# Two blocks of mixed rows turned into row tiles before the input projection ends, and the output projection and second norm in another order of blocks

## The chip, the core and the metric

The kernel runs on one NeuronCore of one Trainium2 chip. The metric is device time in microseconds: the median of repeated executions (three are shown). A separate execution was recorded by the hardware profiler; it shows when each instruction ran on each engine: TensorE (PE, matmuls; its weight loads are shown apart as PEld), VectorE (DVE), ScalarE (ACT), GpSimd (POOL), and SyncE (SP), whose queue starts the DMAs.

## What is computed

One decoder layer on 1024 tokens of width 1024. Cut to its steps:

```python
h = rms_norm(x, norm1_w)
da_q, da_k, da_v, dn_qkv, dn_z, dn_a, dn_b = split(h @ w_in)
# group A: differential attention, 4 heads, causal, two 64-wide softmax maps per head
p = softmax(scale * rms_norm(da_q) @ rms_norm(da_k).T + causal)        # for each of two maps
da_o = rms_norm((p[0] - lam * p[1]) @ da_v, da_out_norm_w) * (1 - lam_init)
# group B: gated DeltaNet, 4 heads: conv + SiLU, decay, chunked delta rule (a scan over the tokens)
dn_o = rms_norm(gated_delta_rule(...), dn_out_norm_w) * silu(dn_z)
mix = concat([da_o, dn_o], axis=-1)                                    # 512 + 512 columns
x = x + mix @ w_out
h = rms_norm(x, norm2_w)
x = x + square(relu(h @ w_up)) @ w_down
```

## The kernel before

Tokens are cut into eight blocks of 128 (`NT`), columns into eight of 128 (`KB`). Float32 products are made of three faster ones: each operand is split into a rounded high half and a low half that holds the rest, and each product runs as high x high, high x low, low x high. That is why three matmul lines always stand together: L994 to L996 in the input projection of attention (`da_units`), L1273 to L1275 in the output projection (`half`), L1434 to L1436 in the MLP's up products.

The left operand is held transposed in two large tiles, `hH` and `hL` (high and low halves, all eight column blocks by all tokens). During the input projection they hold the normed input; afterwards the mixed rows (`mix`, turned) take their place, and after the output projection the rows normed for the MLP. So a column block of `hH` can be overwritten only once the input projection has read it for the last time.

From about 220 us to 620 us of the span, the scan, the attention projection, attention, the output projection and the second norm run interleaved. The order of PE's instructions is written out by a planner (`Interleave`, L40 to L117): each piece of work is a Python generator, a "stream" with a priority; the planner keeps a clock of its own, adds estimated durations, and at each step takes the first stream, in order of priority, whose next step is due. Smaller numbers go first: scan 0, output of the scan 1, loads of mixed rows 1.4, turning of mixed rows 1.5, turning of q and k pieces 1.6, attention values 2, scores 3, input projection 4, turning of normed rows (`backs`) 4.5, output projection 5, first up products 6. PE's order is fixed by this; the framework's scheduler orders the other engines and SP's queue.

The streams that matter here:

- **`da_units`** (input projection for attention, three passes over eight blocks). At the end of the last pass it loads the first quarter of w_out (rows 512 to 1023, columns 0 to 511), `pre`, then sets `state["proj"]`. `da_turns` turns the q and k pieces, 32 in all, counted in `state["turned"]`.
- **`scores`** and **`values`** (attention, in units of one head and one block). `scores` makes both maps' scores in PSUM, takes the maximum (DVE, L1135), the exponential (ACT, L1139) into a tile `pexp` of the pool `ae` (four buffers) or, every third, of `be`, and combines the maps (DVE, L1149). At most three scored units wait in `ready`. `values` transposes the result (L1171), multiplies it with v (L1183), norms it and stores it to `mixa_d`. Head 1 is scored up to block 3 until the projection is done (L1102). The order of units is head 0, head 1 by rising blocks, then heads 2 and 3 together by falling blocks. `state["scored"]` and `state["attn"]` mark the ends of the two streams.
- **`mix_loads`** and **`mixed`**: the scan's rows (`mixn_d`, columns 512 to 1023 of the mix) are loaded block by block into `mt` (two buffers), from block 7 down (`tiles`), transposed on PE (L252), rounded by ACT into `hH` (L261) and split by DVE into `hL` (L262). Then attention's rows (`mixa_d`, columns 0 to 511) likewise, each block when its four heads are stored. After the sixteenth turn, and when attention is done, buffers are given back and `state["free"]` is set.
- **`outproj`** starts when `state["proj"]` and `state["scan"]` are set. `half(kh, w, n, tb)` is twelve matmuls of 512 columns: block `tb`, input half `kh`, output half `n`, accumulated in one of two PSUM banks and added by DVE to the residual row `accs[tb]` (L1280), which was loaded from x. First pass: `kh` = 1 (scan's rows), n = 0 for all eight blocks, then n = 1. Second pass: `kh` = 0 (attention's rows); of the list `todo` the first entry whose rows have been turned is taken. Quarters of w_out are loaded by `load_unit` into two alternating sets of weight tiles; ACT rounds them and POOL splits them (L213, L214).
- **`norm2`** runs behind a block's second n half: it stores the row to `acc_d`, squares it on ACT (L1292), and scales it by DVE into a `pexp` buffer of `ae` (L1298). Before `free` only the first four entries of `tiles` may do so, and only once all is scored.
- **`backs`** turns normed rows once `free` is set (L252 with `hn` for the first four blocks, with a copy into a `kept` tile on ACT, L256, and a split on DVE, L259; `turn_b`, L1366, for the last four). `up_first` makes the first products of the MLP from the first four blocks. Its weights are loaded when the last n = 0 half of the second pass is done.

The residual rows, the kept rows and the first raw up weights share the eight buffers of one tag, "row" (`row_tile`), so each new one waits for the release of the one eight allocations before.

Of the kernel before, what the change touches and what calls it, by code (L numbers as in the profile page):

```python
# [9 lines left out]
F32 = mybir.dt.float32  # L10
# [8 lines left out]
P = 128  # L19
# [113 lines left out]
def tile_hymba_layer(  # L133
# [113 lines left out]
    def to_hT(src, tb, psp, tag, k0=0, nk=KB, keep=None, col=None):  # L247
        sl = slice(tb * P, (tb + 1) * P)
        for g in range(0, nk, 4):
# [4 lines left out]
            ks = slice(k0 + g, k0 + g + 4)  # L254
            if keep is not None:
                S.copy(keep, psv)  # L256
            if col is None:
                S.copy(hH[:, ks, sl], psv)
                V.tensor_tensor(hL[:, ks, sl], psv, hH[:, ks, sl].bitcast(F32), ALU.subtract)  # L259
            else:  # L260
                S.activation(hH[:, ks, sl], psv, AF.Copy, scale=col)  # L261
                V.scalar_tensor_tensor(hL[:, ks, sl], psv, col, hH[:, ks, sl].bitcast(F32), ALU.mult, ALU.subtract)  # L262
# [609 lines left out]
    def scan_out(c, Sold, yy):  # L872
# [40 lines left out]
        if c == NT - 1:  # L913
# [6 lines left out]
            for tb in tiles:  # L920
                accs[tb] = row_tile("acc")
# [8 lines left out]
    def prefetch_x(after):  # L930
        if state["scan"] and state["xs"] < NT:
            tb = state["xs"]
# [3 lines left out]

    late, accs, vts, v_at, qa_free = [], {}, {}, {}, [0.0] * 3
# [136 lines left out]
    ready = []  # L1074

    def scores():
# [6 lines left out]
        for u, (h, tb) in enumerate(order):  # L1083
# [18 lines left out]
            while h == 1 and tb >= 4 and not state["proj"]:  # L1102
                yield flow.now + 100, None
# [11 lines left out]
            pl = n // npc  # L1115
            pe, ssum = [], ap.tile([P, 2], F32, tag="ssum", name="ssum", bufs=4)
            mx = ap.tile([P, 2], F32, tag="mx", name="mx", bufs=4)
            for m in range(2):
# [18 lines left out]
                ep = pools["be"] if state["scan"] and npe % 3 == 0 else ae  # L1137
                e = ep.tile([P, SEQ], F32, tag="pexp", name="pexp")
# [13 lines left out]
            ready.append((h, tb, pe[0], ri, vt, t))  # L1152
# [4 lines left out]
    def values():  # L1157
        for _ in order:
            while not ready or ready[0][5] > flow.now:
                yield (flow.now + 100 if not ready else ready[0][5]), None  # L1160
            h, tb, pe, ri, vt, _t = ready[0]
# [47 lines left out]
    def turn(src, t, tb, k0, keep=None, col=None):  # L1209
        r = yield from flow.bank("px", at=t)  # L1210
        to_hT(src, tb, px, "px", k0, 4, keep, col)
# [12 lines left out]
    def mix_loads():  # L1224
        while not (pre and state["scan"]):
# [9 lines left out]
    def mixed():  # L1235
        while not state["proj"]:
            yield flow.now + 200, None
        for i in range(2 * NT):
            while not loads:
                yield flow.now + 50, None  # L1240
            mt, t, tb, k0 = loads.pop(0)
            yield from turn(mt, t, tb, k0, col=mw[:, 1:2] if k0 else mw[:, 0:1])
# [18 lines left out]
    def outproj():  # L1261
# [4 lines left out]
        def half(kh, w, n, tb):  # L1266
# [3 lines left out]
            ps = pf.tile([P, 512], F32, tag="pf", name="ps_op")  # L1270
            for k in range(4):
                kk = 4 * kh + k
                T.matmul(ps, hH[:, kk, sl], wh[:, k, :], start=(k == 0), stop=False)  # L1273
# [563 lines left out]
```

## Time and profile before

| | us |
|---|---|
| median of the three runs | 1226.28 |
| lowest, highest | 1226.03, 1226.78 |
| profiled execution, whole | 1228.35 |
| its span, first to last instruction | 1226.6 |
| busy in the span: PE, DVE, ACT, POOL | 1212.7, 849.7, 605.4, 120.7 |
| input projection's last matmul (L996) starts | 444.08 |
| first output-projection matmul (L1273) | 450.20 |
| first and last transposition of mixed rows (L252 from mt) | 445.65, 589.93 |
| last attention value matmuls (L1183) | 580.66 |
| last output-projection matmul (L1275) | 607.94 |

The profile was taken on one execution of its own, so times inside it are read against 1226.6 and differences are carried over to the median. Matmuls are pipelined: one is shown from its start to its modelled end, so neighbours overlap. A row of the timeline reads: start, duration, engine, line of the kernel, operation, what it writes from what it reads, shape, count, and in brackets the idle time of the engine just before, with what ended it. In the waits view a row is: who waited, for whom, total, times, longest.

### The profile page before, as it was taken

Reading aid. Unit: us, or ns where it says so; the run is one execution under the profiler, and the core shown is the slowest. Engines: PE = TensorE matmul, PEld = TensorE weight load, DVE = VectorE, ACT = ScalarE, POOL = GpSimd, SP = SyncE. Lnnn points to the kernel's source line nnn. Section 1 sums busy time; section 2 is a strip of 40 time slices with the busy share of each in tenths; the row PEclk is TensorE's granted clock in tenths of the full one; section 3 lists DMA queues with packets and bytes.
Section 4 is the critical chain, followed back from the end, with each engine's and each line's share of the span. In section 5 each row is a group of like instructions: output and inputs, shape, how many; then the busy total and the mean of one; then the engine's idle time right before and its main releaser. Section 6 shows DMA issues by size and latency. Waiting matters only on the chain.

```text
span 1226.6 us, 17630 instructions
## 1 busy us (share of the span) xinstructions
PE 1212.7 (99%) x6331; PEld 1028.6 (84%) x6331; DVE 849.7 (69%) x1445; ACT 605.4 (49%) x1173; POOL 120.7 (10%) x162
## 2 busy tenths in 40 slices
PE   9999999999999999999999999999999999999998
PEld 9988888898788888888788888888888888888887
DVE  7687788478868577766798554565577955786553
ACT  7565544234456555656566444454563333333331
POOL 0011110223332231212100000000000000000000
PEclk9999999999999999999999999999999999999999
DMA  6564442457755674334528433443279855433401
GB/s 229 163 187 129 115 128 83 123 157 242 231 164 176 183 243 137 109 84 144 183 86 282 163 123 137 172 172 137 103 250 345 330 187 184 162 103 103 137 35 69
DMA packets 160783, 199.04 MB, mean 162 GB/s; under 512 B 20960, under 2 KB 120632, under 8 KB 160696
## 3 DMA queue, kind: packets, MB, share of 16 engines
q1 hardware_dynamic: 160696, 197.92, 49.2%
q8 instruction: 50, 0.82, 0.3%
q14 instruction: 37, 0.30, 0.1%
HBM read 132.32 MB, written 65.56 MB: 161 GB/s over the span
## 4 chain that ended last, share of the span: by engine, by line
PE 91%; DVE 3%; DMA 2%; ACT 2%; issue 1%; POOL 0%; SPq 0%; ACTq 0%; POOLq 0%; DVEq 0%
PE X L1436 5%; PE X L1435 5%; PE X L1434 5%; PE X L1750 4%; PE X L1751 4%; PE X L1752 4%; PE ps_dn L221 4%; PE ps_dn L220 4%; PE ps_dn L219 4%; PE ps_qk L994 3%; PE ps_qk L996 3%; PE ps_qk L995 3%; PE Y L1436 3%; PE Y L1435 3%; PE Y L1434 3%; PE ps_o L1183 2%
## 5 line engine op out<-in xcount | busy, mean ns | idle before, releaser
L1353 ACT CAST hH<-ur 128x1024 fp32r<-128x1024 f32 x56 | 58.7, 1050 | 166.0 <-PE X L1751 79.1
L1354 DVE TENSOR_TENSOR hL<-ur,hH 128x1024 fp32r<-128x1024 f32 x56 | 68.3, 1223 | 78.6 <-ACT hH L1353 78.6
L1354 DVE TENSOR_TENSOR op<-raw,op 128x1024 fp32r<-128x1024 f32 x48 | 58.7, 1223 | 75.1 <-PE X L1435 42.1
L1750 PE MATMUL X<-hH 128*128 128x512 f32 x224 | 87.1, 389 | 0.0
L1751 PE MATMUL X<-hL,hH 128*128 128x512 f32 x224 | 87.1, 389 | 0.0
L1752 PE MATMUL X<-hH,hL 128*128 128x512 f32 x224 | 87.1, 389 | 0.0
L994 PE MATMUL ps_qk<-wH,hH 128*128 128x512 f32 x192 | 81.9, 427 | 0.7 <-ACT qn L1022 0.7
L995 PE MATMUL ps_qk<-wL,hH 128*128 128x512 f32 x192 | 75.3, 392 | 1.2 <-DVE wL L214 1.2
L219 PE MATMUL ps_dn<-hH,wH 128*128 128x512 f32 x192 | 75.9, 395 | 0.0
L220 PE MATMUL ps_dn<-hL,wH 128*128 128x512 f32 x192 | 75.6, 394 | 0.0
L996 PE MATMUL ps_qk<-wH,hL 128*128 128x512 f32 x192 | 75.5, 393 | 0.0
L221 PE MATMUL ps_dn<-hH,wL 128*128 128x512 f32 x192 | 75.4, 393 | 0.0
L1354 DVE TENSOR_TENSOR hL<-dw,hH 128x1024 fp32r<-128x1024 f32 x56 | 68.2, 1219 | 2.8 <-ACT hH L1353 2.7
L1353 ACT CAST op<-raw 128x1024 fp32r<-128x1024 f32 x48 | 50.5, 1052 | 34.7 <-PE Y L1436 19.9
L1353 ACT CAST hH<-dw 128x1024 fp32r<-128x1024 f32 x56 | 58.6, 1047 | 16.7 <-PE X L1752 5.2
L1139 ACT ACTIVATE pexp<-ps_sc,mx 128x128 f32<-128x128 f32 (+7 forms) x64 | 47.3, 741 | 26.3 <-DVE mx L1135 26.2
L577 DVE SCALAR_TENSOR_TENSOR cy<-cp,pv,cy 128x512 f32<-128x512 f32 x72 | 53.9, 748 | 8.4 <-ACT cy L575 7.5
L1135 DVE TENSOR_REDUCE mx<-ps_sc 128x1 f32<-128x128 f32 (+7 forms) x64 | 47.5, 754 | 14.2 <-PE ps_sc L1133 13.7
L1273 PE MATMUL ps_op<-wH,hH 128*128 128x512 f32 x128 | 53.6, 419 | 0.0
L1275 PE MATMUL ps_op<-wH,hL 128*128 128x512 f32 x128 | 50.3, 393 | 0.0
L1274 PE MATMUL ps_op<-wL,hH 128*128 128x512 f32 x128 | 50.0, 391 | 0.0
L1434 PE MATMUL Y<-hH,op 128*128 128x512 f32 x128 | 49.8, 389 | 0.0
(355 smaller groups left out, 3382.3 us busy)
## 6 DMA issues: line engine op xcount, KB each, us to landing
ur<-ud SPq DMA_DIRECT2D x28, 1024.0 KB, 5.0
raw<-in_w_up_dram SPq DMA_DIRECT2D x32, 512.0 KB, 3.8
dw<-in_w_down_dram SPq DMA_DIRECT2D x32, 512.0 KB, 7.2
qk_d<-qa SPq DMA_DIRECT2D x32, 256.0 KB, 2.7
ud<-ua SPq DMA_DIRECT2D x16, 512.0 KB, 4.0
ud<-s SPq DMA_DIRECT2D x16, 512.0 KB, 2.6
wraw<-in_w_in_dram SPq DMA_DIRECT2D x24, 256.0 KB, 3.3
wraw<-in_w_in_dram SPq DMA_DIRECT2D x48, 128.0 KB, 2.6
```

The source lines that it names most:

```text
L219: T.matmul(ps, lh(k), rh(k), start=(k == 0), stop=False)
L220: T.matmul(ps, lh(k), rl(k), start=False, stop=False)
L221: T.matmul(ps, ll(k), rh(k), start=False, stop=(k == n - 1))
L994: T.matmul(ps, hH[:, 4 * kh + k, sl], wh[:, k, :], start=(kh + k == 0), stop=False)
L995: T.matmul(ps, hH[:, 4 * kh + k, sl], wl[:, k, :], start=False, stop=False)
L996: T.matmul(ps, hL[:, 4 * kh + k, sl], wh[:, k, :], start=False, stop=(kh + k == 4))
L1353: S.copy(dst[0], src)
L1354: V.tensor_tensor(dst[1], src, dst[0].bitcast(F32), ALU.subtract)
L1434: T.matmul(ps, op[0][:, k, cs], h[0][:, k, :], start=start and k == 0, stop=False, skip_group_check=True)
L1750: T.matmul(o, v[0][:, j, sl], v[2][:, j, c], start=s0, stop=False, skip_group_check=True)
L1751: T.matmul(o, v[0][:, j, sl], v[3][:, j, c], start=False, stop=False, skip_group_check=True)
L1752: T.matmul(o, v[1][:, j, sl], v[2][:, j, c], start=False, stop=s1, skip_group_check=True)
```

## The change

It does four things. (1) The first two blocks of the scan's rows, blocks 7 and 6, are turned before the input projection has ended, not into `hH` and `hL` but into two of the eight row tiles (`first_rows`; the high half of a tile's columns takes the rounded part, the other the rest); their loads start when the scan is done and more than 20 of the q and k pieces are turned. (2) Since these two row tiles are taken, only six rows of x are loaded ahead, in the order of `tiles`; the rows for the last two blocks are allocated and loaded after the four halves that read the two tiles. (3) The first pass of the output projection runs in an order written out by hand, and the second takes both halves of the first four blocks ahead of the last four's first halves; a norm before `free` has to wait, in the planner, until no scored unit that has not been read holds the `ae` buffer that it will take. (4) Head 1's block 4 may be scored before the projection is done. The number and kinds of the matmuls stay the same.

```diff
--- before.py
+++ after.py
@@ -244,7 +244,7 @@
         V.tensor_scalar(t, ss, scale, eps, ALU.mult, ALU.add)
         G.tensor_tensor(o, t, neghalf[:, :n], ALU.pow)
 
-    def to_hT(src, tb, psp, tag, k0=0, nk=KB, keep=None, col=None):
+    def to_hT(src, tb, psp, tag, k0=0, nk=KB, keep=None, col=None, dst=None):
         sl = slice(tb * P, (tb + 1) * P)
         for g in range(0, nk, 4):
             ps = psp.tile([P, 512], F32, tag=tag, name="ps_tr")
@@ -252,14 +252,15 @@
                 T.transpose(ps[:, j * P:(j + 1) * P], src[:, (g + j) * P:(g + j + 1) * P], ident)
             psv = ps.rearrange("p (k t) -> p k t", k=4)
             ks = slice(k0 + g, k0 + g + 4)
+            dh, dl = dst or (hH[:, ks, sl], hL[:, ks, sl])
             if keep is not None:
                 S.copy(keep, psv)
             if col is None:
-                S.copy(hH[:, ks, sl], psv)
-                V.tensor_tensor(hL[:, ks, sl], psv, hH[:, ks, sl].bitcast(F32), ALU.subtract)
+                S.copy(dh, psv)
+                V.tensor_tensor(dl, psv, dh.bitcast(F32), ALU.subtract)
             else:
-                S.activation(hH[:, ks, sl], psv, AF.Copy, scale=col)
-                V.scalar_tensor_tensor(hL[:, ks, sl], psv, col, hH[:, ks, sl].bitcast(F32), ALU.mult, ALU.subtract)
+                S.activation(dh, psv, AF.Copy, scale=col)
+                V.scalar_tensor_tensor(dl, psv, col, dh.bitcast(F32), ALU.mult, ALU.subtract)
 
     pctx = ctx.enter_context(ExitStack())
     pj = pctx.enter_context(tc.tile_pool(name="pj", bufs=2, space=PSUM))
@@ -917,7 +918,9 @@
             spctx.close()
             mp = ctx.enter_context(tc.tile_pool(name="mp", bufs=1, **left))
             pools["mp"] = mp
-            for tb in tiles:
+            for tb in tiles[:2]:
+                first_rows[tb] = mp.tile([P, DM], F32R, tag="row", name="first", bufs=8)
+            for tb in tiles[:6]:
                 accs[tb] = row_tile("acc")
             pools["a2"] = bctx.enter_context(tc.tile_pool(name="a2", bufs=1, **left))
             pools["be"] = bctx.enter_context(tc.tile_pool(name="be", bufs=2, **left))
@@ -928,12 +931,13 @@
         return pools["mp"].tile([P, DM], F32, tag="row", name=name, bufs=8)
 
     def prefetch_x(after):
-        if state["scan"] and state["xs"] < NT:
-            tb = state["xs"]
+        if state["scan"] and state["xs"] < NT - 2:
+            tb = tiles[state["xs"]]
             state["xs"] += 1
             with tc.issue_after(after.ins):
                 nc.sync.dma_start(accs[tb], x2[tb * P:(tb + 1) * P, :])
 
+    first_rows = {}
     late, accs, vts, v_at, qa_free = [], {}, {}, {}, [0.0] * 3
 
     def da_turns():
@@ -1071,7 +1075,7 @@
 
     order = [(0, t) for t in range(NT)] + [(1, t) for t in range(NT)]
     order += [(h, t) for t in reversed(range(NT)) for h in (2, 3)]
-    ready = []
+    ready, in_ae = [], [0]
 
     def scores():
         heads, loaded, npe, nsc, since = {}, {}, 0, 0, 0
@@ -1099,7 +1103,7 @@
                 loaded[3] = max(flow.now, loaded[2]) + 6000
             if q is None and h > 0:
                 q = load_q(h, tb)
-            while h == 1 and tb >= 4 and not state["proj"]:
+            while h == 1 and tb >= 5 and not state["proj"]:
                 yield flow.now + 100, None
             yield loaded.get(h, 0.0), None
             if q is None:
@@ -1113,6 +1117,7 @@
             n = (tb + 1) * P
             npc = 1 if n <= 512 else 2
             pl = n // npc
+            mine = []
             pe, ssum = [], ap.tile([P, 2], F32, tag="ssum", name="ssum", bufs=4)
             mx = ap.tile([P, 2], F32, tag="mx", name="mx", bufs=4)
             for m in range(2):
@@ -1135,6 +1140,8 @@
                 V.tensor_reduce(mx[:, m:m + 1], scv, axis=AX.XY, op=ALU.max, negate=True)
                 npe += 1
                 ep = pools["be"] if state["scan"] and npe % 3 == 0 else ae
+                mine.append(in_ae[0] if ep is ae else 1e9)
+                in_ae[0] += ep is ae
                 e = ep.tile([P, SEQ], F32, tag="pexp", name="pexp")
                 S.activation(e[:, :n].rearrange("p (a b) -> p a b", a=npc), scv, AF.Exp, bias=mx[:, m:m + 1],
                              accum_out=ssum[:, m:m + 1])
@@ -1149,7 +1156,7 @@
             V.scalar_tensor_tensor(pe[0][:, :n], pe[1][:, :n], cf, pe[0][:, :n], ALU.mult, ALU.add)
             t = flow.chain(vec(10), vec(1, 60), vec(n, 100), start=t - flow.HOP)
             q = load_q(*order[u + 1]) if u + 1 < len(order) and order[u + 1][0] // 2 < state["da"] else None
-            ready.append((h, tb, pe[0], ri, vt, t))
+            ready.append((h, tb, pe[0], ri, vt, t, mine[0]))
         state["scored"] = True
 
     turn_no = [0]
@@ -1158,7 +1165,7 @@
         for _ in order:
             while not ready or ready[0][5] > flow.now:
                 yield (flow.now + 100 if not ready else ready[0][5]), None
-            h, tb, pe, ri, vt, _t = ready[0]
+            h, tb, pe, ri, vt, _t, _ = ready[0]
             while v_at.get(tb, 1e12) > flow.now:
                 yield flow.now + 50, None
             vt = vt or vts[0]
@@ -1206,9 +1213,9 @@
     tiles = list(reversed(range(NT)))
     landed, hns = {}, {}
 
-    def turn(src, t, tb, k0, keep=None, col=None):
+    def turn(src, t, tb, k0, keep=None, col=None, dst=None):
         r = yield from flow.bank("px", at=t)
-        to_hT(src, tb, px, "px", k0, 4, keep, col)
+        to_hT(src, tb, px, "px", k0, 4, keep, col, dst)
         flow.pe(4 * TR)
         t = flow.chain(*[act(512)] * (1 if keep is None else 2), vec(512))
         flow.hold(r, t)
@@ -1222,7 +1229,7 @@
     loads = []
 
     def mix_loads():
-        while not (pre and state["scan"]):
+        while not (state["scan"] and state["turned"] > 20):
             yield flow.now + 200, None
         for i in range(2 * NT):
             t = tiles[i % NT]
@@ -1233,13 +1240,14 @@
             loads.append((mt, flow.now + (MIX_T if i < NT else MIX_A), t, 4 if i < NT else 0))
 
     def mixed():
-        while not state["proj"]:
-            yield flow.now + 200, None
         for i in range(2 * NT):
-            while not loads:
+            while not loads or i == 2 and not state["proj"]:
                 yield flow.now + 50, None
             mt, t, tb, k0 = loads.pop(0)
-            yield from turn(mt, t, tb, k0, col=mw[:, 1:2] if k0 else mw[:, 0:1])
+            if i < 2:
+                first_rows[tb] = [x.rearrange("p (k t) -> p k t", k=4) for x in
+                                  (first_rows[tb][:, 0:512], first_rows[tb][:, 512:1024])]
+            yield from turn(mt, t, tb, k0, col=mw[:, 1:2] if k0 else mw[:, 0:1], dst=first_rows[tb] if i < 2 else None)
             state["mixed"] += 1
         while not state["attn"]:
             yield flow.now + 50, None
@@ -1268,11 +1276,11 @@
             (wh, wl), wt = w
             r = yield from flow.bank("pf", at=wt[0])
             ps = pf.tile([P, 512], F32, tag="pf", name="ps_op")
+            lh, ll = first_rows[tb] if kh and tb in first_rows else [x[:, 4 * kh:4 * kh + 4, sl] for x in (hH, hL)]
             for k in range(4):
-                kk = 4 * kh + k
-                T.matmul(ps, hH[:, kk, sl], wh[:, k, :], start=(k == 0), stop=False)
-                T.matmul(ps, hH[:, kk, sl], wl[:, k, :], start=False, stop=False)
-                T.matmul(ps, hL[:, kk, sl], wh[:, k, :], start=False, stop=(k == 3))
+                T.matmul(ps, lh[:, k, :], wh[:, k, :], start=(k == 0), stop=False)
+                T.matmul(ps, lh[:, k, :], wl[:, k, :], start=False, stop=False)
+                T.matmul(ps, ll[:, k, :], wh[:, k, :], start=False, stop=(k == 3))
                 flow.pe(648)
                 if k < 3:
                     yield wt[k + 1], None
@@ -1285,6 +1293,7 @@
         def norm2(tb, pos):
             w2b = pools["w2b"] if state["free"] else w2b0
             hn = ae.tile([P, SEQ], F32, tag="pexp", name="hn2")
+            in_ae[0] += 1
             hn = [hn[:, 0:512], hn[:, 512:1024]]
             ss = laid("nss")
             nc.sync.dma_start(acc_d[tb], accs[tb])
@@ -1301,30 +1310,39 @@
 
         w0 = pre[0]
         w1 = load_unit(w_out_v, [(512, 512)], 4, 4), unit_time()
-        while state["xs"] < NT:
-            tb = state["xs"]
-            state["xs"] += 1
-            nc.sync.dma_start(accs[tb], x2[tb * P:(tb + 1) * P, :])
-        for n in range(2):
-            for tb in tiles:
-                while landed.get((tb, 4), 1e12) > flow.now:
-                    yield min(landed.get((tb, 4), 1e12), flow.now + 100), None
-                yield from half(1, (w0, w1)[n], n, tb)
-            w = load_unit(w_out_v, [(512 * n, 512)], 0, 4), unit_time()
-            if n == 0:
-                w0 = w
-            else:
-                w1 = w
+        def rows_of_x(upto):
+            while state["xs"] < upto:
+                tb = tiles[state["xs"]]
+                state["xs"] += 1
+                nc.sync.dma_start(accs[tb], x2[tb * P:(tb + 1) * P, :])
+
+        rows_of_x(NT - 2)
+        for n, i in [(0, 0), (0, 1), (0, 2), (0, 3), (1, 0), (1, 1), (0, 4), (0, 5), (1, 2), (1, 3), (0, 6), (0, 7),
+                     (1, 4), (1, 5), (1, 6), (1, 7)]:
+            tb = tiles[i]
+            while landed.get((tb, 4), 1e12) > flow.now:
+                yield min(landed.get((tb, 4), 1e12), flow.now + 100), None
+            yield from half(1, (w0, w1)[n], n, tb)
+            if (n, i) == (1, 1):
+                for x in tiles[6:]:
+                    accs[x] = row_tile("acc")
+                rows_of_x(NT)
+            if i == NT - 1:
+                w = load_unit(w_out_v, [(512 * n, 512)], 0, 4), unit_time()
+                if n == 0:
+                    w0 = w
+                else:
+                    w1 = w
         aw = dctx.enter_context(tc.tile_pool(name="aw", bufs=1, **right))
         w2b0 = aw.tile([P, DM], F32, name="w2b0")
         nc.sync.dma_start(w2b0, norm2_w.partition_broadcast(P))
-        todo = [(n, i) for n in range(2) for i in range(NT)]
+        todo = [(n, i) for g in range(2) for n in range(2) for i in range(4 * g, 4 * g + 4)]
         left0 = NT
         flow.add(6, up_first())
         flow.add(4.5, backs())
         while todo:
             j = next((j for j, (n, i) in enumerate(todo) if landed.get((tiles[i], 0), 1e12) <= flow.now
-                      and (n == 0 or (0, i) not in todo) and (n == 0 or state["scored"] and i < 4 or state["free"])), None)
+                      and (n == 0 or (0, i) not in todo) and (n == 0 or state["free"] or state["scored"] and i < 4 and all(in_ae[0] - 4 < x[6] for x in ready))), None)
             if j is None:
                 yield flow.now + 50, None
                 continue
```

## The prediction

> **What bounds the kernel now.** First the page's list of engines, then the windows view over four stages of the span (its columns: length, then busy time and count of PE, PE's weight loads, DVE, ACT and POOL, the granted clock, the DMA share, GB/s).
>
> ```profile
> PE 1212.7 (99%) x6331; PEld 1028.6 (84%) x6331; DVE 849.7 (69%) x1445; ACT 605.4 (49%) x1173; POOL 120.7 (10%) x162
> ```
> ```profile
> 10.00:300.00 290.00, 289.01 (x1827) 253.56 (x1826) 224.90 (x524) 146.72 (x408) 44.84 (x57) 1.00 0.50 149
> 300.00:620.00 320.00, 312.61 (x1794) 267.75 (x1793) 232.58 (x536) 188.38 (x488) 74.11 (x94) 1.00 0.56 169
> 620.00:1200.00 580.00, 580.00 (x2561) 480.23 (x2560) 381.99 (x371) 262.62 (x269) 0.00 (x0) 1.00 0.47 167
> ```
>
> TensorE bounds it. It stands idle 13.9 us of 1226.6, and 7.4 us of that lie between 300 and 620 us, where the change works. The change adds and removes no instruction of TensorE, so what it can win is idle time there. Next, the waits view of PE: the whole list of what it waited for is short, and these are its rows that lie behind 437 us, where the input projection ends, or sum over it (total, times, longest).
>
> ```profile
> PE ps_sc L1130 <- ACT pexp L1139: 1.5, 2, 0.9
> ...
> PE ps_tr L1366 <- DVE hL L259: 0.9, 1, 0.9
> ...
> PE ps_at L1171 <- ACT om L1189: 0.5, 1, 0.5
> PE ps_at L1171 <- DVE hL L262: 0.4, 1, 0.4
> ...
> PE ps_tr L1366 <- ACT hn L1367: 0.3, 1, 0.3
> PE ps_tr L252 <- DVE hL L259: 0.3, 1, 0.3
> ```
>
> The timeline of PE shows how long such a wait really is:
>
> ```profile
> 444.31 0.31 PE L1130 MATMUL ps_sc<-KS,qa 128*128 128x320 f32 x1
> ...
> 448.07 0.22 PE L1133 MATMUL ps_sc<-caus,identr 128*128 128x128 f32 x1
> 449.20 0.44 PE L1130 MATMUL ps_sc<-KS,qa 128*128 128x384 f32 x1 [0.91 <-ACT pexp L1139]
> ...
> 450.20 0.48 PE L1273 MATMUL ps_op<-wH,hH 128*128 128x512 f32 x1
> ```
> ```profile
> 607.71 0.39 PE L1274 MATMUL ps_op<-wL,hH 128*128 128x512 f32 x1
> 607.94 0.39 PE L1275 MATMUL ps_op<-wH,hL 128*128 128x512 f32 x1
> 609.26 0.63 PE L1366 MATMUL ps_tr<-ident,hn 128*128 128x128 f32 x4 [0.94 <-DVE hL L259]
> ```
>
> Undisturbed, a matmul of 512 columns starts 0.23 us behind the last though it is shown 0.39 long, so the next could start 0.16 before the shown end. A wait costs its shown idle time and about 0.16 more: the one at 609.26 costs 0.94 + 0.16 = 1.10. I take 0.16 for all. The places are: **front**, behind the projection, 1.5 + 2 x 0.16 = 1.82; **middle**, a transposition held by the split of mixed rows (0.4), 0.56; **tail**, 1.10 + 0.46 + 0.46 = 2.02; and the 0.5 behind ACT om, 0.66, which no edit addresses.
>
> **The change part by part.**
>
> *Two mixed blocks turned early.* Eight transpositions, two ACT roundings and two DVE splits move from 445 us to about 372 (the planner's count of 21 turned pieces is met near 363, where PE's timeline has the 21st pair of L947 and L948, and it allows 8 us, MIX_T, for the loads).
>
> ```profile
> 445.65 1.04 PE L252 MATMUL ps_tr<-ident,mt 128*128 128x128 f32 x8
> ```
> ```profile
> 447.12 1.26 ACT L261 ACTIVATE hH<-ps_tr,mw 128x512 fp32r<-128x512 f32 x2
> ```
> ```profile
> 445.47 1.56 DVE L1135 TENSOR_REDUCE mx<-ps_sc 128x1 f32<-128x640 f32 x2
> ...
> 447.84 0.74 DVE L262 SCALAR_TENSOR_TENSOR hL<-ps_tr,mw,hH 128x512 fp32r<-128x512 f32 x1
> ```
> ```profile
> L1232 SPq DMA_DIRECT2D mt<-mixn_d x8: 377/472/2327, 356.1 to 467.6; - x8
> ```
>
> PE pays 1.04 there instead of here: zero net. The first load of mt was issued at 356.1 already, so the two loads are no new traffic; the next two, issued at 446.7 before, follow the early turns and leave the busiest DMA time. DVE gives up 2 x 0.74 = 1.48 and ACT 1.26 in a stretch where DVE is full:
>
> ```profile
> 420.00:430.00 10.00, 10.00 (x54) 8.48 (x53) 3.76 (x14) 4.17 (x12) 2.35 (x4) 1.00 0.44 138
> ...
> 440.00:450.00 10.00, 8.51 (x48) 7.34 (x47) 8.04 (x16) 7.29 (x15) 3.49 (x5) 1.00 0.89 277
> 450.00:460.00 10.00, 10.00 (x54) 8.46 (x54) 9.71 (x18) 5.79 (x13) 3.47 (x3) 1.00 0.98 296
> ```
>
> *One score unit more ahead of the projection's end* (block 4 of head 1, the gate moved from 4 to 5). Its ten matmuls, 444.31 to 445.65 = 1.34 on PE, and on DVE 1.56 for the maxima move to about 425, where DVE is busy 3.76 of 10 and PE has projection matmuls that only slide by 1.34. Together DVE loses 3.0 us from 444 to 460, out of 16 at most, and attention is one unit ahead.
>
> *Output projection at once.* Before, its first matmul stands at 450.20, behind transposition, split and two score units that queue for one another. Now its first two blocks need only w_out. Six to twelve matmuls of 0.23 (1.4 to 2.8 us) are there for the 1.82 of the front: **gain 1.82**. Bounds: nothing, if the planner puts them elsewhere, and 1.82. The middle wait comes from mixed turns that share two px banks with attention; two turns fewer stand there: I take half, **0.28** (0 to 0.56).
>
> *x rows of the last two blocks late.* They wait for the four halves that read the row tiles, and are then two DMAs on SP, with attention's query loads and stores behind them in the queue.
>
> ```profile
> acc<-in_x_dram SPq DMA_DIRECT2D x8, 512.0 KB, 3.8
> ```
>
> Four halves, 4 x 12 x 0.23 = 11.0 us of PE, come between their issue and the half that needs the first: 3.8 is covered, cost nothing. If they were issued 7 us late, DVE's addition would stand, with all of DVE behind it.
>
> *Four blocks finished ahead.* Before, three blocks are normed before the last mixed rows are turned (589.93) and the fourth at 593.5; the copy of its rows into the kept tile then stood on its own store:
>
> ```profile
> 593.50 1.40 DVE L1298 SCALAR_TENSOR_TENSOR hn<-acc,nr,w2b 128x512 f32<-128x512 f32 x2
> ```
> ```profile
> 607.32 0.59 ACT L256 COPY kept<-ps_tr 128x512 f32<-128x512 f32 x1 [0.65 <-DMA acc_d<-acc]
> ```
>
> That copy leads to the split for which PE waited until 609.26. With second halves of the first four blocks chosen before the first halves of blocks 4 to 6, all four norms lie before 589.9 and the store is issued some 8 us earlier. Then all eight transpositions of normed rows can run at once and the first up products (24 matmuls, 5.5 us) stand ready to cover the rest. I take the 1.10 and one of the 0.46 as gone, **1.56** (0 to 2.02). The norm gate holds the planner only. By its count of buffers the first norm asks that the last unit but two has been read, the second that the last but one has:
>
> ```profile
> 567.87 0.38 PE L1171 MATMUL ps_at<-ident,pexp 128*128 128x128 f32 x2
> ...
> 569.92 0.27 PE L1171 MATMUL ps_at<-ident,pexp 128*128 128x128 f32 x1
> ...
> 571.77 0.48 PE L1273 MATMUL ps_op<-wH,hH 128*128 128x512 f32 x1
> ```
>
> On before's timeline they are read by 567.9 and 569.9, and the first two such halves start right behind the one and at 571.77: cost 0 (to 0.5, if the order puts the half first).
>
> *New waits.* PE's order is redealt from 372 to 620 and the other engines' with it. I set one more wait of the size of the 0.66 row: **+0.66**; bounds 0 and, with the w_out weights, 5.0 (below).
>
> Sum: 1.82 + 0.28 + 1.56 - 0.66 = **3.0 us less**. The profiled execution took 1228.35 (1226.6 of span and 1.75 around it); it becomes 1225.35. The median of the runs lies 2.07 below the profiled one: 1226.28 - 3.0 = **1223.3 us**.
>
> **The rivals.**
>
> *A. More goes than that*: all of front, middle and tail, and nothing new: -4.4, 1221.9; with the 0.66 as well, 5.1, 1221.2. For it: DVE is relieved where it is fullest.
>
> *B. Attention's end does not move.* The last rows come by a chain that more work ahead of the output projection does not shorten:
>
> ```profile
> 580.66 0.39 PE L1183 MATMUL ps_o<-vt,at 128*128 128x128 f32 x2
> ...
> 589.50 0.39 PE L1275 MATMUL ps_op<-wH,hL 128*128 128x512 f32 x1
> 589.93 0.63 PE L252 MATMUL ps_tr<-ident,mt 128*128 128x128 f32 x4
> ```
>
> At 589.50 PE did the last half that it had (the 27th of 32) and 0.2 us later the rows came: a supply exactly used up. If attention keeps its times, 2.1 us saved ahead become 2.1 us of idleness at 587. What is left is the tail: 1226.28 - 1.56 = 1224.7. Against it: attention starts a unit ahead and gets DVE time.
>
> *C. The last rows come later; slower than before.* DVE works in order, and the last unit's scale stood behind a norm:
>
> ```profile
> 582.25 0.68 DVE L1280 TENSOR_TENSOR acc<-acc,ps_op 128x512 f32<-128x512 f32 x1
> 582.84 1.41 DVE L1298 SCALAR_TENSOR_TENSOR hn<-acc,nr,w2b 128x512 f32<-128x512 f32 x2
> 584.17 0.15 DVE L244 TENSOR_SCALAR oft<-so 128x1 f32<-128x1 f32 x1
> ```
>
> A half's addition (0.68) and a norm (1.41) cost it 2.1 together. Four norms before the end instead of three, bunched by the new order, could put two more there: 4.2 later. With PE's supply used up, PE waits all of it, and the front's gain is lost as in B: 1226.28 + 4.2 - 1.56 = 1228.9. It decides from the point where more than one additional norm stands ahead of that scale.
>
> *D. The second half of w_out late.* It is split by POOL; this row is its last two pieces:
>
> ```profile
> 458.99 2.54 POOL L214 TENSOR_TENSOR wL<-wraw,wH 128x512 fp32r<-128x512 f32 x2 [6.53 <-ACT wH L213]
> ```
> ```profile
> L214 POOL TENSOR_TENSOR wL<-wraw,wH x12: 1269/1292/1471, 449.7 to 556.7; 128x512 fp32r<-128x512 f32 x12
> ```
>
> It is whole at 461.5. Before, it is needed behind eight halves; now behind four. At the earliest that is 444.31 + 1.34 + 11.0 = 456.7, a wait of 4.8 with scores and transpositions behind it: 1223.3 + 4.8 = 1228.1. Against it: attention and turns fill part of these 11 us (before, four halves took from 450.20 to the row below), and fewer DMAs compete for the second pair of pieces.
> ```profile
> 465.50 0.40 PE L1275 MATMUL ps_op<-wH,hL 128*128 128x512 f32 x1
> ```
>
> [...]
>
> *E. The early turns do not get early*: the scan's end or the planner's clock holds them back. Speaks against it: mt is loaded from 356.1. Then it is the case of B, and counted there.
>
> **How the numbers follow.** About 0.2%, 2.45 us, is what a measurement of this kernel can tell from no change. Forecast 0.50 (0.42 of it faster by over 0.2%, 0.08 within); A 0.12, faster; B 0.16 (0.01 faster, 0.15 within); D 0.10 (0.07 within, 0.03 slower); C 0.12 (0.03 within, 0.09 slower). Faster 0.55, within 0.33, slower 0.12. The range reaches below A's last bound by 0.4, for waits too short for the list, and stops at 1228.3 above, past D's price; it leaves out C's upper part and D's late end: 1220.8 to 1228.3.
>
> **What would show it.** Right: transpositions of mt near 372 us; output-projection matmuls within 1 us of the projection's last; no PE wait of 0.9 on pexp at 447; four norm pairs before the last mt transposition, and no ACT wait on the acc_d store; span near 1223.6. Wrong: PE idle ahead of the last mt transposition (B, C), or at the first matmul on the second half of w_out (D), or several new waits of 0.5 between 450 and 580.

## The result: slower by half a per cent

| | before | after |
|---|---|---|
| median, us (six runs each) | 1226.43 | 1233.26 |
| lowest to highest | 1225.63 to 1227.31 | 1230.41 to 1235.48 |
| ratio of the two | | 1.0054, 95% interval 1.0044 to 1.0065 |
| profiled execution | 1228.35 | 1235.48 |

The forecast was 1223.3, with a range to 1228.3: the sign was wrong, and the time lies 5 us outside. The list of engines on the page of the changed kernel, and the windows view of its middle stage:

```profile
PE 1213.9 (98%) x6331; PEld 1031.9 (84%) x6331; DVE 849.7 (69%) x1445; ACT 605.9 (49%) x1173; POOL 124.4 (10%) x162
```
```profile
300.00:620.00 320.00, 307.56 (x1750) 265.45 (x1749) 226.64 (x524) 184.15 (x479) 77.28 (x93) 0.98 0.53 162
```

The work is the same, 6331 matmuls, but where PE idled 7.4 us of these 320 it now idles 12.4, and the granted clock, 1.00 before, is 0.98. The waits view of PE over that stretch names two places (and a third row, for later):

```profile
PE ps_tr L252 <- issue: 3.9, 1, 3.9
PE ps_at L1178 <- DVE qa L959: 3.1, 2, 2.9
...
PE ps_tr L252 <- ACT om L1196: 0.4, 1, 0.4
```

**The later place.** PE's timeline, then ACT's, then those of SP and POOL:

```profile
462.66 0.60 PE L252 MATMUL ps_tr<-ident,mt 128*128 128x128 f32 x4
467.14 1.09 PE L252 MATMUL ps_tr<-ident,mt 128*128 128x128 f32 x4 [3.88 <-issue]
```
```profile
461.90 0.62 ACT L213 CAST wH<-wraw 128x512 fp32r<-128x512 f32 x1 [0.97 <-DMA wraw<-in_w_out_dram]
462.43 0.47 ACT L958 ACTIVATE qa<-ps_qkt,qw 64x256 fp32r<-64x256 f32 x1
465.41 0.62 ACT L213 CAST wH<-wraw 128x512 fp32r<-128x512 f32 x1 [2.52 <-DMA wraw<-in_w_out_dram]
466.05 0.47 ACT L958 ACTIVATE qa<-ps_qkt,qw 64x256 fp32r<-64x256 f32 x1
```
```profile
460.25 0.38 SPq L1064 DMA_DIRECT2D vt<-v_d  x1
460.72 4.05 SPq L211 DMA_DIRECT2D wraw<-in_w_out_dram  x2
```
```profile
459.24 1.29 POOL L214 TENSOR_TENSOR wL<-wraw,wH 128x512 fp32r<-128x512 f32 x1 [1.16 <-ACT wH L213]
```

Read upwards from PE. "Issue" names nobody, so ask which bank the second turn of mixed rows writes: one of two px banks. Its last user was the q/k turn of 460.36, and ACT must read that twice (L958), each time with DVE behind it (L959). ACT's first reading was at 462.43, the second only at 466.05 (DVE's at 466.55), because in ACT's order the rounding of a piece of w_out (second quarter) stood between them, idle for 2.52 us until its DMA landed. The piece is the first of the two in SP's row. There are two raw buffers, so it could be issued only when POOL's split had freed one (459.24 + 1.29 = 460.53). From its issue at 460.72 it took about 4.7 to land, where these loads take 2.9 in the median of this run; a load of 512 KB (vt) had been issued just ahead of it, but whether that is the reason is not shown. The rest of the 4.05 is SP waiting for the next free buffer; it held up the queue, not this piece. ACT of the kernel before had the same roundings, but behind the readings of the turn:

```profile
456.02 0.47 ACT L954 ACTIVATE qa<-ps_qkt,qw 64x256 fp32r<-64x256 f32 x1 [1.76 <-DVE qa L955]
456.52 0.69 ACT L261 ACTIVATE hH<-ps_tr,mw 128x512 fp32r<-128x512 f32 x1
458.29 0.62 ACT L213 CAST wH<-wraw 128x512 fp32r<-128x512 f32 x1 [1.09 <-DMA wraw<-in_w_out_dram]
```

**The earlier place** is much like it, with the last pieces of w_in, but here DVE is a link of the chain too. PE's timeline, ACT's and DVE's:

```profile
392.76 0.63 PE L1178 MATMUL ps_at<-ident,pexp 128*128 128x128 f32 x4 [2.86 <-DVE qa L959]
```
```profile
389.69 0.62 ACT L213 CAST wH<-wraw 128x512 fp32r<-128x512 f32 x1 [0.89 <-DMA wraw<-in_w_in_dram]
390.33 0.47 ACT L958 ACTIVATE qa<-ps_qkt,pv 64x256 fp32r<-64x256 f32 x1
```
```profile
390.34 0.69 DVE L214 TENSOR_TENSOR wL<-wraw,wH 128x512 fp32r<-128x512 f32 x1 [0.89 <-ACT wH L213]
390.95 1.14 DVE L1156 SCALAR_TENSOR_TENSOR pexp<-pexp,cf 128x896 f32<-128x896 f32 x1
392.12 0.49 DVE L959 SCALAR_TENSOR_TENSOR qa<-ps_qkt,pv,qa 64x256 fp32r<-64x256 f32 x1
```

The bank's last user was the q/k turn of 385.79. ACT's second reading of it came at 390.33, behind a rounding that had waited for its piece. DVE's order had the split of the same piece next, and it waited for the rounding; only behind the split and a combination of maps (L1156) did DVE read the bank for the last time, until 392.61. One late piece thus held two engines.

**And then the clock.** Windows around both places, cut where the granted clock (third number from the end) changes:

```profile
390.74:394.15 3.41, 1.39 (x9) 1.25 (x9) 3.01 (x5) 1.84 (x5) 0.00 (x0) 1.00 0.47 160
394.15:397.56 3.41, 3.41 (x10) 2.53 (x9) 1.08 (x3) 1.04 (x2) 0.71 (x2) 0.50 0.66 203
397.56:400.97 3.41, 3.41 (x25) 3.11 (x24) 1.56 (x2) 1.22 (x3) 0.91 (x1) 1.00 0.66 198
462.42:465.83 3.41, 0.84 (x6) 0.50 (x4) 2.03 (x3) 0.89 (x3) 1.81 (x1) 1.00 0.68 210
465.83:469.24 3.41, 2.10 (x8) 2.00 (x9) 1.49 (x3) 2.04 (x4) 1.26 (x1) 0.50 0.78 236
469.24:472.66 3.42, 3.42 (x11) 2.87 (x10) 2.68 (x3) 1.10 (x2) 0.00 (x0) 0.50 0.35 125
```

Behind each wait PE gets half the clock for one or two stretches of 3.41 us. The bill for the profiled execution: two waits, 2.86 + 3.88 + 2 x 0.16 = 7.1; half clock over 10.24 us, of which PE worked 8.93 (3.41 + 2.10 + 3.42), 4.5; together 11.5. Against it stand the gains of front and tail (below), 1.8 + 1.2. That is +8.5, and +7.1 was measured, so the bill is 1.4 too high: half of PE's busy time is a rough price for the half clock (matmuls of 512 columns start 0.43 us apart in it, 394.56 to 394.99, instead of 0.23), and other small waits came and went (one behind ACT's qn at 311 grew from 0.7 to 1.7, the 0.5 behind ACT om is gone); I do not divide the rest. The clock also goes, roughly, with the spread of the six runs: mean granted clocks from 0.998 (1230.41) to 0.994 (1235.48). At this price a half-clock stretch with PE busy costs 3.41 x 0.5 = 1.7 us, and 0.0014 of the mean clock (1.7 of 1233.8); 0.004 is about three of them, 5.1 us, and the two runs differ by 5.07. Only the run of 1235.48 has a trace (with a fourth such stretch at 8.45, ahead of anything that was changed), so this reading is not shown; one execution of g4 below has a mean clock of 0.949 on record at 1224.81, which it does not explain.

### The profile page after: what moved, and what is told of

The parts are those of the page before. It is cut to its first block, busy times and chain, and to the rows that moved or that the text cites. A ratio compares the mean times of both kernels' runs of the same rounds, so it can differ in the third digit from the quotient of the medians.

```text
span 1233.8 us, 17625 instructions
## 1 busy us (share of the span) xinstructions
PE 1213.9 (98%) x6331; PEld 1031.9 (84%) x6331; DVE 849.7 (69%) x1445; ACT 605.9 (49%) x1173; POOL 124.4 (10%) x162
## 4 chain that ended last, share of the span: by engine, by line
PE 89%; DVE 3%; issue 3%; DMA 3%; ACT 2%; POOL 1%; SPq 0%; DVEq 0%; ACTq 0%; POOLq 0%
PE X L1453 5%; PE X L1454 5%; PE X L1452 5%; PE X L1768 4%; PE X L1770 4%; PE X L1769 4%; PE ps_dn L219 4%; PE ps_dn L220 4%; PE ps_dn L221 4%; PE ps_qk L998 3%; PE Y L1454 3%; PE Y L1453 3%; PE Y L1452 2%; PE ps_qk L1000 2%; PE ps_qk L999 2%
## 5 line engine op out<-in xcount | busy, mean ns | idle before, releaser
L213 ACT CAST wH<-wraw 128x512 fp32r<-128x512 f32 x64 | 37.2, 623 | 27.6 <-DMA wraw<-in_w_in_dram 15.5
L1452 PE MATMUL Y<-hH,op 128*128 128x512 f32 x128 | 49.8, 389 | 0.0
L1454 PE MATMUL Y<-hH,op 128*128 128x512 f32 x128 | 49.8, 389 | 0.0
L1453 PE MATMUL Y<-hL,op 128*128 128x512 f32 x128 | 49.8, 389 | 0.0
```

Of the source, the lines that this page charges most:

```text
L1452: T.matmul(ps, op[0][:, k, cs], h[0][:, k, :], start=start and k == 0, stop=False, skip_group_check=True)
L1453: T.matmul(ps, op[0][:, k, cs], h[1][:, k, :], start=False, stop=False, skip_group_check=True)
L1454: T.matmul(ps, op[1][:, k, cs], h[0][:, k, :], start=False, stop=stop and k == 3, skip_group_check=True)
```

## The experiments

The main theory: *a rounding in ACT's order, waiting for a late weight piece, holds up what PE needs; PE then idles for 2 to 4 us and gets half the clock.* Rivals: the early turns' load itself, the new order itself, or a slow stretch with a cause of its own. Each time stands against runs of the kernel before on the same chip.

| run | median, us | ratio to before, 95% interval |
|---|---|---|
| e1, second pass alone | 1226.46 | 1.0007, 0.9998 to 1.0016 |
| e2, early turns undone | 1233.69 | 1.0058, 1.0045 to 1.0070 |
| e4, PE's waits filled | 1231.13 | 1.0038, 1.0026 to 1.0051 |
| e5, eight roundings on POOL | 1227.74 | 1.0014, 1.0005 to 1.0023 |
| f1, score gate alone | 1237.91 | 1.0099, 1.0084 to 1.0114 |
| f2, first-pass order alone | 1233.66 | 1.0060, 1.0047 to 1.0073 |
| f3, second pass undone | 1234.04 | 1.0068, 1.0054 to 1.0082 |
| f4, mended | 1224.20 | 0.9987, 0.9977 to 0.9997 |
| g1, f2 with roundings on POOL | 1231.57 | 1.0040, 1.0028 to 1.0052 |
| g2, before with roundings on POOL | 1225.90 | 0.9997, 0.9989 to 1.0006 |
| g3, f4 with more on POOL | 1224.59 | 0.9986, 0.9976 to 0.9995 |
| g4, g3 with the old gate | 1225.36 | 0.9993, 0.9985 to 1.0001 |

**e5: take the roundings out of ACT's order.** PE's order stays the same, instruction by instruction.

```diff
-            S.copy(wh[:, k:k + st, :], raw)
+            rnd.tensor_copy(wh[:, k:k + st, :], raw) if rnd else S.copy(wh[:, k:k + st, :], raw)
...
-            return load_unit(src, ranges, k0, 4, eng=V), unit_time("V", 610.0)
+            return load_unit(src, ranges, k0, 4, eng=V, rnd=G if ranges[0][0] == 1280 and k0 == 4 else None), unit_time("V", 610.0)
...
-        w1 = load_unit(w_out_v, [(512, 512)], 4, 4), unit_time()
+        w1 = load_unit(w_out_v, [(512, 512)], 4, 4, rnd=G), unit_time()
```

> Changed kernel with eight roundings of weight pieces (the last half unit of w_in, and the second quarter of w_out) moved from ACT to POOL; PE's order is the same instruction by instruction. Main theory: a rounding that waits for a late DMA stands in ACT's order ahead of a q/k turn's rounding, this keeps the px bank, PE waits for the bank and then gets half the clock. Then both waits shrink to under 0.5 and the clock stays at 1.00: 1222.5 to 1224. Rival: DVE (which reads the same bank after ACT) or the DMAs hold the bank anyway: waits stay over 2 us, 1231 to 1234.

Some 5 us came back, and the clock is 1.00 from 300 to 620. PE's waits view, 300 to 640, has among others:

```profile
PE ps_qk L999 <- DVE wL L214: 2.5, 3, 1.3
...
PE ps_tr L252 <- issue: 1.1, 1, 1.1
...
PE ps_qk L998 <- POOL wH L213: 0.8, 1, 0.8
```

The wait of 3.88 is 1.1, that of 2.86 is gone from ps_at. The time expected was missed by about 4: on POOL the pieces of w_in came late for the projection itself (the first row, of which 1.0 stood there before, and the third). At the earlier place PE now waits 0.82, 0.23 and 1.28 for them, 2.3 together instead of 2.86, in pieces behind which the clock held. So ACT's order was the holder at the later place; at the earlier one, with the turns where they are, the late pieces keep PE waiting whoever rounds them.

**e4: fill the waits with work.** 40 transpositions of the identity (`warm` is 24 for the fifth turn of mixed rows), into banks that the real turns overwrite.

```diff
+            for _ in range(warm):
+                T.transpose(ps[:, 0:P], ident, ident)
             for j in range(4):
                 T.transpose(ps[:, j * P:(j + 1) * P], src[:, (g + j) * P:(g + j + 1) * P], ident)
...
+            for _ in range(16 if i == 23 else 0):
+                T.transpose(pt[:, 0:P], ident, ident)
             T.transpose(pt[:, 0:P], qn[:, 0:P], ident)
```

> Changed kernel plus 40 transpositions of the identity on PE (16 ahead of the q/k turn at 389.5, 24 ahead of the turn of mixed rows at 462.7), written into banks that these turns overwrite; about 0.11 us each, 4.4 us of more work, PE's order otherwise the same. If the clock falls because PE stood idle for 3 to 4 us, the waits shrink to about 1.1 and 1.4, the granted clock stays at 1.00 in 393 to 400 and 467 to 473, and 3 to 4.5 us come back: about 1229.5, faster with more work. If the slow stretch has another cause, nothing comes back (1233.3), and if the idle time was not really there to be filled, it is up to 4.4 slower (1237.7).

More work, and about 2 us less time (the intervals just overlap). Windows in the trace of e4:

```profile
389.77:393.18 3.41, 2.39 (x13) 2.08 (x14) 2.50 (x5) 2.28 (x5) 0.00 (x0) 1.00 0.62 211
393.18:396.60 3.42, 3.42 (x24) 3.02 (x23) 1.86 (x4) 0.78 (x3) 1.62 (x2) 1.00 0.61 204
461.49:464.90 3.41, 1.06 (x10) 0.85 (x9) 0.56 (x2) 1.77 (x3) 1.23 (x1) 1.00 0.23 76
464.90:468.32 3.42, 3.42 (x13) 3.12 (x12) 1.73 (x3) 0.69 (x1) 0.04 (x1) 0.50 0.74 232
```

At the first place the idle time fell to 1.2 and the clock held. At the second 2.3 us were left instead of 1.4, and the clock fell for one stretch instead of two. So in this run the clock followed PE's own idleness: it held behind a stretch of 3.41 us with 1.02 idle and fell behind one with 2.35.

**e2: which part brings the waits?** The early turns undone, everything else kept.

```diff
-        while not (state["scan"] and state["turned"] > 20):
+        while not (pre and state["scan"]):
...
-            while not loads or i == 2 and not state["proj"]:
+            while not loads or not state["proj"]:
```

> Changed kernel with the first two blocks turned where they were turned before (behind the input projection, loads issued there), still into the row tiles; order of the output projection and score gate kept. If the two long PE waits (2.86 at 392.8, 3.88 at 467.1) come from the early turns and their loads, both go and the tail gain stays: about 1225. If they come from the output projection's order or from the score unit that was moved, the second wait stays, with the slow clock behind it: 1229 to 1231.

A miss for the simple form of the rival: the wait at 390 is gone, so the early turns brought that one, but the time is the same. Others have come, near 448 and 470:

```profile
PE ps_sc L1135 <- DMA qa<-qk_d: 2.9, 1, 2.9
...
PE ps_sc L1135 <- DMA wraw<-in_w_out_dram: 1.1, 1, 1.1
```
```profile
452.39 7.35 SPq L211 DMA_DIRECT2D wraw<-in_w_out_dram  x3
```

SP stood 7.35 us over three pieces of w_out, and what stood behind them in its queue had to wait; the queries for which PE waited at 471 were issued at 466.67.

**f1: the score gate alone**, in the kernel before.

```diff
-            while h == 1 and tb >= 4 and not state["proj"]:
+            while h == 1 and tb >= 5 and not state["proj"]:
```

> Kernel before with one part alone: head 1's block 4 may be scored before the projection is done (gate 5 for 4). As predicted it costs nothing and takes some of the wait for pexp behind the projection: 1225 to 1226.4. If it is this unit that moves the last q/k turns behind the roundings of the second quarter of w_out, a PE wait of 2 us or more stands near 460, with a clock of 0.50 behind it: 1230 or more.

The part that I had costed at nothing is the dearest alone: 11.8. PE's timeline, SP's and ACT's in f1:

```profile
473.16 0.77 PE L1130 MATMUL ps_sc<-KS,qa 128*128 128x512 f32 x1 [5.76 <-DMA qa<-qk_d]
```
```profile
465.77 2.28 SPq L1232 DMA_DIRECT2D mt<-mixn_d  x1
468.17 0.54 SPq L1067 DMA_DIRECT2D qa<-qk_d  x1
```
```profile
630.88 0.62 ACT L1353 CAST wH<-wraw 128x512 fp32r<-128x512 f32 x1 [3.80 <-DMA wraw<-in_w_up_dram]
```

The largest wait begins with SP's order this time: the queries were issued only at 468.17, behind a load that held the queue for 2.28. PE started on them 4.99 behind that (473.16), where this load takes 2.7 to land in the median of the changed kernel's trace. A second wait, 2.5 at 630, is ACT behind a piece of w_up. A stretch at 0.50 follows both, at 471.68 and at 632.11. The place foretold (460) was wrong, the kind right.

**f2: the first-pass order alone**, in the kernel before (its loop replaced by the list of the diff above).

> Kernel before with one part alone: the hand-written order of the output projection's first pass (two halves on the second quarter of w_out after four, instead of after eight). If this order is what brings the wait (the second quarter of w_out needed sooner, rival D of the prediction), PE waits some us for wL or wH at the first n = 1 half: 1228 to 1231. If not, it stays within 1 us of 1226.

Slower, as rival D had it, but not by its mechanism: PE never waits for the second quarter at an output half. ACT's timeline in f2 shows what stands ahead of attention's copies:

```profile
525.17 0.62 ACT L213 CAST wH<-wraw 128x512 fp32r<-128x512 f32 x1 [1.54 <-DMA wraw<-in_w_out_dram]
527.95 0.62 ACT L213 CAST wH<-wraw 128x512 fp32r<-128x512 f32 x1 [2.16 <-DMA wraw<-in_w_out_dram]
528.47 0.26 ACT L1189 COPY om<-ps_o 128x128 f32<-128x128 f32 x1
...
552.83 0.62 ACT L213 CAST wH<-wraw 128x512 fp32r<-128x512 f32 x1 [3.89 <-DMA wraw<-in_w_out_dram]
```

PE waited 1.8 and 2.1 for them, and 2.4 at 622 behind a piece of w_up. **g1** puts the twelve roundings of w_out's later quarters on POOL (`rnd=G` on those units):

> Kernel before with the new order of the first pass alone, and all twelve roundings of w_out's later quarters moved from ACT to POOL (PE's order the same as with the order alone, 1233.7). Main theory: the order costs only through roundings in ACT's order that wait for late pieces; the two waits of 2.0 at 527 and 2.2 at 554 go, the one of 2.6 at 622 (behind an up weight, still on ACT) stays: 1228 to 1230. If the order itself is slow, 1233 or more.

Both waits are gone, and 2 us (the intervals just overlap), but two new ones came (0.7 at 536, 1.3 at 568), so it is 1.6 above what was expected and still about 5 above the kernel before; the one at 622 stayed, as foretold:

```profile
PE ps_tr L1368 <- ACT hn L1369: 2.5, 1, 2.5
...
PE ps_tr L252 <- ACT om L1189: 1.3, 1, 1.3
PE ps_at L1171 <- DVE hL L262: 0.7, 1, 0.7
```

**e1: the second pass alone**, in the kernel before (`todo` and the norm gate).

> Kernel before with one part of the change alone: the order of the output projection's second pass (four blocks finished ahead) and the norm gate that belongs to it. If the tail gain is as the prediction had it, 1.56 us go: 1224.9 against 1226.4 of the kernel before, and the ACT wait on the store of acc_d (0.65 at 607) is gone. If the two long waits of the changed kernel come from this order, it shows them and comes out at 1230 or more.

No gain. The wait in the tail did not go but grew; ACT and PE in e1:

```profile
604.81 0.59 ACT L256 COPY kept<-ps_tr 128x512 f32<-128x512 f32 x1 [0.36 <-DMA acc_d<-acc]
```
```profile
606.75 0.63 PE L1370 MATMUL ps_tr<-ident,hn 128*128 128x128 f32 x4 [1.51 <-DVE hL L259]
```

What released the copy was still the store of acc_d, so the wait that the edit was to remove is smaller on ACT (0.36 instead of 0.65) but not gone. **f3** undoes this part in the changed kernel:

> Changed kernel with the second pass in the order of before (first halves of all eight blocks ahead of second halves). If the tail gain of the prediction is real inside the changed kernel, this is 1 to 2 us slower than the changed kernel: 1234.3 to 1235.3. If, as the run of the second pass alone said, it is worth nothing, 1233.3 within 0.7.

0.0014 above the changed kernel's ratio, with intervals that overlap: it stays open whether the order is worth 1 or nothing there.

**f4: two mends together**: only the second quarter of w_out rounded on POOL, and the early turns behind the last pieces of w_in.

```diff
-        while not (state["scan"] and state["turned"] > 20):
+        while not (state["scan"] and state["turned"] > 24):
...
-        w1 = load_unit(w_out_v, [(512, 512)], 4, 4), unit_time()
+        w1 = load_unit(w_out_v, [(512, 512)], 4, 4, rnd=G), unit_time()
```

> Changed kernel with two mends: the four roundings of the second quarter of w_out on POOL instead of ACT, and the early turns after 24 q/k turns instead of 20 (near 412 instead of 377), behind the last weight pieces of the projection. By the main theory both long waits shrink below 1.3, the granted clock stays at 1.00 throughout, and the front gain remains: 1224 to 1226, below the run with eight roundings on POOL (1227.7), where PE waited 3 us for the pieces of w_in. If the re-dealt order itself costs time whatever ACT does, it stays at 1228 or more.

9 us below the changed kernel, and 0.13% (1.6 us) below the one before, about half of the 3.0 forecast; how much each of the two mends brings was not measured apart. No stretch of half clock between 300 and 620: the trace's mean granted clock is 1.000, and one stretch would take 0.0014 of it. The waits did not get as short as expected. PE's waits view, from 360 on, is led by

```profile
PE ps_tr L252 <- issue: 1.9, 1, 1.9
PE ps_at L1178 <- ACT om L1196: 1.5, 1, 1.5
PE ps_tr L252 <- DMA mt<-mixa_d: 1.0, 1, 1.0
```

**Controls.** Does the gain belong to POOL alone, and is the gate harmful in itself?

> Kernel before, unchanged but for the same twelve roundings on POOL. In its trace no long wait of PE stands behind a rounding of w_out, so the theory expects no gain: 1225.5 to 1227. If it gains 2 or more, the gain of the mended kernel (1224.2) belongs to POOL and not to the change.

> The mended kernel (early turns after 24 q/k turns, second quarter of w_out rounded on POOL) with the last two quarters on POOL too. Its trace had no long wait behind those two, so about the same: 1223.5 to 1225.

> The kernel of the run before this one with the score gate put back to 4. The gate alone made the kernel before 11.8 slower; if that was the gate's own work, this is faster by some us (1219 to 1222); if it was only where the roundings and loads fell, it is within 1.5 of the run with gate 5 (1222.5 to 1226).

As expected in all three: POOL gives the kernel before nothing, so the gain of f4 needs the change; the last two quarters add nothing; and the gate that cost 11.8 alone makes no difference that can be measured here. It cost by where things fell, not by its work. A third raw buffer, which should let SP issue sooner, was not tried.

## Why the prediction was wrong

**The failed step** is "New waits": "one more wait of the size of the 0.66 row; bounds 0 and 5.0". By the bill above they came to about 11.5 in the profiled execution. Two errors are in it. The bound priced one wait at a time, on one resource, while the redealt order moved the roundings on ACT and the loads on SP as well, and one late piece held both ACT and DVE. And a wait was priced as its length; the half clock behind it, 4.5 of the 11.5, was not in the sum.

- *Front, 1.82: right.* No PE wait on pexp remains behind the projection. The first output matmul stands at 456.19, 2.7 behind the projection's last (453.51) instead of under 1, but eight transpositions and ten score matmuls fill the gap without idling.
- *Tail, 1.56: the size about right, the reason not.* PE's busy time from 600 to 640 went from the first to the second of these rows (before, after), 1.2 more, and no ACT copy waits for the store of acc_d. But two norm pairs lie before the last turn of mixed rows (593.28), not four, and alone the edit won nothing (e1).

```profile
600.00:640.00 40.00, 38.49 (x190) 31.33 (x189) 36.31 (x58) 27.31 (x50) 2.00 (x3) 1.00 0.45 145
```
```profile
600.00:640.00 40.00, 39.67 (x201) 32.80 (x200) 34.28 (x60) 27.35 (x58) 2.51 (x4) 1.00 0.45 145
```

- *Middle, 0.28: the row is gone, the place is worse.* PE no longer waits for a split of mixed rows (0.4 before, at 462.49), but the 3.88 stands at the same two px banks. The 0.4 in the third row of the waits above is another one, behind ACT om at 565.79.
- *Early turns, "zero net": wrong by the first place,* 2.86 + 0.16 and about 1.7 of clock, which e2 removes with them. The turns came at 376.7, near the 372 foretold.
- *The score unit "only slides": wrong,* 11.8 alone (f1), nothing in g4.
- *Rivals B and C did not come.* Between 468 and the last turn of mixed rows (593.28) PE's longest wait is that 0.4.
- *Rival D had the resource, not the victim.* The second quarter of w_out was late, but for ACT's and SP's queues; PE never waited for it. No run shows D's late end, which the range leaves out: in the changed kernel POOL's four splits of that quarter took 1.30, 1.29, 1.81 and 1.26, and it was whole at 467.36 instead of 461.5, yet no output half waited. "Who else stands behind the late piece" was the question to ask, and the one I asked only of DVE (rival C).

## What to carry to other kernels

When an order is redealt, list what waits for a DMA on each engine and queue (ACT stood 2.52 us over one piece here, SP 7.35 over three in e2), and ask what would stand behind it in the new order: the weight roundings on ACT, harmless before, cost most here. Keep such conversions on an engine that PE does not depend on for its banks, if it delivers the pieces in time (in e5 it did not for w_in). Price a PE wait at its length and, where 2 us or more of it can fall into one cell of 3.41 us, as in six cells of these traces (below), at about 1.7 more for each stretch at half clock, an estimate from 3.41 x 0.5.

## What the hardware showed

In the trace of the changed kernel the granted clock changes at 8.45, 11.86, 394.15, 397.56, 465.83 and 472.66, all whole multiples of 3.413 us apart (394.15 to 465.83 is 71.68, 21 x 3.413), and has two values, 1.00 and 0.50. I call a stretch of 3.41 us between such times a cell. As far as the cells show, the clock went with PE's idle time within one of them (its length less PE's busy time). Six full-clock cells with 2.0 us or more idle are each followed by one at 0.50: 2.02 and 2.57 in the changed kernel, 3.41 and 2.00 in f1, 2.55 in f3, 2.35 in e4. Between 1.6 and 2.0 it went both ways: 1.66 (changed kernel, at 308.82), 1.74 (f1), 1.75 (g4) and 1.91 (f3) kept the clock, and 1.71 and 1.78 (both e2) lost it. From 300 to 640 us, no full-clock cell with less than 1.66 idle lost it in the traces of the kernels before and after; waits of 2.4 in f2 and 2.5 in g1 cost no clock either (mean of both traces 1.000). So a wait of the same length cost once or twice: in f3 the wait at 390 (2.9 as well) fell across a boundary, with 1.00 idle in one cell and 1.91 in the next, and kept its clock:

```profile
385.87:389.28 3.41, 2.41 (x12) 1.75 (x10) 1.88 (x7) 2.19 (x4) 1.01 (x1) 1.00 1.03 300
389.28:392.70 3.42, 1.51 (x9) 1.36 (x10) 2.90 (x5) 1.91 (x4) 0.00 (x0) 1.00 0.47 157
392.70:396.11 3.41, 3.41 (x20) 2.85 (x19) 1.47 (x4) 1.19 (x3) 1.23 (x2) 1.00 0.78 214
```
